# Convolution taps all on VectorE, the decay products a block pair later, and three steps of the mixers behind each gate chunk, in a hybrid decoder trunk

## The chip, the cores and the metric

The kernel runs on one core of a Trainium2 chip. The metric is device time in microseconds of one execution, and the median over several runs. Before the change three runs gave 1257.48, 1259.5 and 1262.86 us, a median of 1259.5 us.

A core has five engines that each work through their own list of instructions in order: TensorE (PE, whose weight loads the profile lists as PEld), VectorE (DVE), ScalarE (ACT), GpSimd (POOL) and SyncE (SP, which issues DMAs here). They wait for one another by semaphores.

## The reference

Two layers, 256 tokens, width 1024, all weights float32. Each layer is a half-step SwiGLU feed-forward, a mixing sub-layer with three branches, and a second feed-forward:

```python
for l in range(DEPTH):                                   # DEPTH = 2
    x = x + FFN_RESID * swiglu_ffn(rms_norm(x, ffn1_norm[l]), ffn1_w_in[l], ffn1_w_out[l])
    h = rms_norm(x, mix_norm[l])
    uv, c_q, c_kv, k_rope, z, xbc, dt_raw, gates = jnp.split(h @ w_in[l], IN_OFFSETS, axis=-1)
    y_a = gmlp_mixer(uv, ...)
    y_b = mla_mixer(c_q, c_kv, k_rope, cos, sin, ...)    # attention, 8 heads
    y_c = ssd_mixer(z, xbc, dt_raw, ...)                 # state-space scan
    g = jax.nn.sigmoid(gates).reshape(bsz, s, N_BRANCH, D_MODEL)
    merged = sum of g[:, :, i] * (y_i @ w_branch[l, i])
    x = x + merged @ w_out[l]
    x = x + FFN_RESID * swiglu_ffn(rms_norm(x, ffn2_norm[l]), ffn2_w_in[l], ffn2_w_out[l])
```

The state-space branch begins with a causal convolution over time with four taps, one filter for each of 1024 features, and a Silu. Its scan needs, for each of 8 heads and each of two chunks of 128 tokens, the decay matrix `exp(segsum(dt * a))`, a 128x128 triangle of exponentials of running sums:

```python
xbc = lax.conv_general_dilated(xbc, conv_w[:, None, :], (1,), [(SSD_CONV - 1, 0)], ...)   # SSD_CONV = 4
xbc = jax.nn.silu(xbc + conv_b)
dt = jax.nn.softplus(dt_raw + dt_bias)
lmat = jnp.exp(segsum(da))                               # da = dt * -exp(a_log)
```

## The kernel before, in words

**Products.** Every float32 weight chunk (128 partitions x up to 1024 columns, "sub") is loaded by SP into `raw` and split in two parts that TensorE takes at its fast rate: ACT casts the upper part (`whi`, L175) and DVE subtracts it to get the rest (`wlo`, L176). Four buffers hold each part, and the splits run three subs ahead of their use. A product is then three matmuls: L215 to L217 for feature-major results (128 features x 256 tokens), L221 to L223 for token-major ones (128 tokens x up to 512 columns). PE works in order, so a split that is late stops it.

**The mixing sub-layer**, function `mix`, has these stages on PE: eight 128-feature blocks of the convolution's input, in four pairs `i` (ps_in); two halves of the token-major v part (ps_v, 276 columns); seven steps `n` over pairs of middle blocks (`MID_PAIRS`; ps_in again: the latents of the attention for n < 3, then z and u); three and two sub-chunks for q and k/v; 24 chunks of the gates (ps_g); and the merge.

**The convolution.** DVE scales each pair of blocks into `xp` (L587, L589), ACT applies the last tap and the bias into `xbc`, and the other three taps are added in place. For the first block of each pair, `b == 0`, DVE does it with one instruction a tap (L596). For the second block POOL does it with two: a product into the tile `tap` (L599) and a sum (L600). ACT's Silu (L602) takes four blocks at a time. Behind it on ACT come the casts of later subs.

**The steps of the mixers.** All that is not a product with streamed weights is written as generators that yield, and `pump(n)` takes n steps of the first one in the list `work`. The state-space generator `ssd` has as its first step the softplus chain of small DVE instructions (L631 to L654), as its second the high and low parts of da (`dahi` L656, `dalo` L657), the products ps_s and ps_c (L667, L674), and then four steps that each make one decay product: `aseg` (L682, one half on DVE with `dahi`, one on POOL with `dalo`, three buffers), two matmuls into ps_sg (L687, L688) and ACT's exponential (L689). `pump(3)` stands behind each of the seven middle steps (L853), `pump(2 + n % 2)` behind each gate chunk `n` (L1037). By n = 2 the latents' squares are summed on POOL (L847) and turned over by the small product ps_css (L822). In the gate chunks the steps belong to the attention: POOL takes inverse roots for keys and queries (`rs_k`, `rs_q`, L301), multiplies the normed keys and queries (`qk`, L938 and L928), and PE transposes them (ps_t, L965).

**What sets the order.** The program states dependencies and buffers; a scheduler orders the instructions on each engine by its own estimate of time and by priority, where splits have high priority. So a step that is pumped elsewhere can also move instructions of other kinds. POOL issues its DMAs (the feed-forward's summed weights, L166, and accumulating ones, L169) in the same list as its arithmetic.

Of the kernel before, what the change touches and what calls it, by code (L numbers as in the profile page):

```python
# [10 lines left out]
F32 = mybir.dt.float32  # L11
# [4 lines left out]
ALU = mybir.AluOpType  # L16
# [3 lines left out]
P = 128  # L20
DEPTH = 2
SEQ = 256
# [86 lines left out]
def tile_trunk(ctx, tc, wst, xtok, xT, pos, pcol, prow, wsT, cst, out):  # L109
    nc = tc.nc  # L110
    act, dve, pool, pe = nc.scalar, nc.vector, nc.gpsimd, nc.tensor
# [4 lines left out]
    tp = ctx.enter_context(tc.tile_pool(name="tp", bufs=2))  # L116
# [5 lines left out]
    starts, o = [], 0  # L122
# [84 lines left out]
    def next_sub():  # L207
        i = st["use"]
        prefetch(AHEAD + 1)
        st["use"] += 1  # L210
        return splits.pop(i)

    def mm3(ps, whi, wlo, xhl, first, last):

        pe.matmul(ps, lhsT=whi, rhs=xhl[:, 0], start=first, stop=False)  # L215
        pe.matmul(ps, lhsT=whi, rhs=xhl[:, 1], start=False, stop=False)  # L216
        pe.matmul(ps, lhsT=wlo, rhs=xhl[:, 0], start=False, stop=last)  # L217

    def mm3x(ps, xhi, xlo, whi, wlo, first, last, again=False):

        pe.matmul(ps, lhsT=xhi, rhs=whi, start=first, stop=False, skip_group_check=again)  # L221
        pe.matmul(ps, lhsT=xhi, rhs=wlo, start=False, stop=False, skip_group_check=again)  # L222
        pe.matmul(ps, lhsT=xlo, rhs=whi, start=False, stop=last, skip_group_check=again)  # L223
# [89 lines left out]
    def halves(b):  # L313
        return slice(P * b, P * (b + 1))
# [231 lines left out]
    def mix(l, nrm, nxt, late, row, ws):  # L546
        col = pc[:, l]
        qn, kvn = col[:, 24:27], col[:, 27:29]
        cw = col[:, 29:61].rearrange("p (b i) -> p b i", i=4)
# [4 lines left out]
        def blocks(n=2):  # L554

            ps = acc.tile([P, 2, SEQ], F32, name="ps_in", tag="acc")
            for half in range(n):
                hi, lo = next_sub()
                for k in range(KD):
                    s = slice(P * k, P * (k + 1))  # L560
                    mm3(ps[:, half], hi[:, s], lo[:, s], nrm.hl[:, k], k == 0, k == KD - 1)
            return ps
# [3 lines left out]
        for i in range(4):  # L566
            if i == 0:

                pss = [acc.tile([P, SEQ], F32, name="ps_in", tag="acc") for _ in range(2)]
                subs = [next_sub() for _ in range(2)]  # L570
                for part in range(2):
                    for ps, (hi, lo) in zip(pss, subs):
                        for k in range(4 * part, 4 * part + 4):
                            s = slice(P * k, P * (k + 1))
                            mm3(ps, hi[:, s], lo[:, s], nrm.hl[:, k], k == 0, k == KD - 1)
                    if part == 0:
                        late()
                        nrm.finish(True)
                        R = nrm.R
                        R2 = R.unsqueeze(1).broadcast_to([P, 2, SEQ])  # L580
            else:
                ps = blocks()
            xp = tp.tile([P, 2, SEQ + 4], F32, name="xp", tag="xp")
            pool.memset(xp[:, :, 0:3], 0.0)
            if i == 0:
                for b in range(2):
                    dve.tensor_tensor(xp[:, b, 3 : SEQ + 3], pss[b], R, ALU.mult)  # L587
            else:
                dve.tensor_tensor(xp[:, :, 3 : SEQ + 3], ps, R2, ALU.mult)  # L589
            for b in range(2):  # L590
                f = 2 * i + b
                o = xbc[:, f]
                act.activation(o, xp[:, b, 3 : SEQ + 3], AF.Identity, scale=cw[:, f, 3:4], bias=cb_[:, f : f + 1])
                for w in range(3):
                    if b == 0:
                        dve.scalar_tensor_tensor(o, xp[:, b, w : w + SEQ], cw[:, f, w : w + 1], o, ALU.mult, ALU.add)  # L596
                    else:
                        c = tp.tile([P, SEQ], F32, name="tap", tag="sq")
                        pool.tensor_tensor(c, xp[:, b, w : w + SEQ], cw[:, f, w : w + 1].broadcast_to([P, SEQ]), ALU.mult)  # L599
                        pool.tensor_tensor(o, o, c, ALU.add)  # L600
        for i in range(2):
            act.activation(xbc[:, 4 * i : 4 * i + 4], xbc[:, 4 * i : 4 * i + 4], AF.Silu)  # L602
        xsT, bT, cT = xbc[:, 0:4], xbc[:, 4:6], xbc[:, 6:8]
# [4 lines left out]
        for half in range(2):  # L608
            pst = [acc.tile([P, VW], F32, name="ps_v", tag="acc") for _ in range(2)]
            k = 0  # L610
            for n in (3, 3, 2):
                hi, lo = next_sub()
                for i in range(n):
                    for b in range(2):
                        s, w = slice(P * b, P * (b + 1)), slice(VW * i, VW * (i + 1))
# [193 lines left out]
        def pump(n):  # L809
            while work and n > 0:  # L810
                try:
                    next(work[0])
                    n -= 1
                except StopIteration:
                    work.pop(0)

        def c_norm():
            ps = mxp.tile([P, 4], F32, name="ps_css", tag="mx")
            for i in range(2):
                for b in range(2):  # L820
                    c = 2 * i + b
                    pe.matmul(ps[:, c : c + 1], lhsT=css[:, i, P * b : P * (b + 1)], rhs=ones[:, 0:1], start=True, stop=True)  # L822
            m = tp.tile([P, 4], F32, name="ms_c", tag="ms4")
            dve.tensor_scalar(m[:, 0:2], ps[:, 0:2], 1.0 / 384, EPS, ALU.mult, ALU.add)
            dve.tensor_scalar(m[:, 2:4], ps[:, 2:4], 1.0 / 256, EPS, ALU.mult, ALU.add)
            r = tp.tile([P, 4], F32, name="rs_c", tag="rsc", bufs=1)
            pool.tensor_tensor(r, m, mhalf[:, :4], ALU.pow)
            return r

        for n, (a, b) in enumerate(MID_PAIRS):  # L830
            ps = blocks(b - a)[:, : b - a]
            Rn = R2[:, : b - a]
            if n < 3:
                cr = tp.tile([P, 2, SEQ], F32, name="craw", tag="t")
                dve.tensor_tensor(cr[:, : b - a], ps, Rn, ALU.mult)
                for k in range(a, b):
                    c = cr[:, k - a]
                    g = qn[:, k : k + 1] if k < 3 else kvn[:, k - 3 : k - 2]
                    act.activation(chi[:, k], c, AF.Copy, scale=g)
                    dve.scalar_tensor_tensor(clo[:, k], c, g, chi[:, k].bitcast(F32), ALU.mult, ALU.subtract)  # L840
                    to = css[:, 0 if k < 3 else 1]
                    if k in (0, 3):
                        act.activation(to, c, AF.Square)
                    else:
                        sq = tp.tile([P, SEQ], F32, name="csq", tag="sq")
                        act.activation(sq, c, AF.Square)
                        pool.tensor_tensor(to, to, sq, ALU.add)  # L847
            else:
                dve.tensor_tensor(zt[:, a - 5 : b - 5] if n < 5 else ut[:, a - 9 : b - 9], ps, Rn, ALU.mult)
            if n == 2:  # L850
                rc = c_norm()
            done["z"] = n >= 4
            pump(3)  # L853


        big = bp.tile([P, 2, 2, H, QK], F32, name="qk", tag="big12a")
# [5 lines left out]
        for k in range(3):  # L862
            hi, lo = next_sub()
            for b in range(2):
                s = slice(P * b, P * (b + 1))
                for i in range(2):
                    w = slice(384 * i, 384 * (i + 1))
                    mm3x(psq[b][i], chi[:, k, s], clo[:, k, s], hi[:, w], lo[:, w], k == 0, k == 2)
        for b in range(2):
            for i in range(2):  # L870
                o = q[:, b, 4 * i : 4 * i + 4].rearrange("p h d -> p (h d)")
# [6 lines left out]
        for k in range(2):  # L878
            hi, lo = next_sub()
            for b in range(2):  # L880
                s = slice(P * b, P * (b + 1))
                for i in range(2):
                    w = slice(512 * i, 512 * (i + 1))
# [142 lines left out]
        n = 0  # L1026
        for h in range(2):
            for i in range(3):
                ps = [acc.tile([P, HD], F32, name="ps_g", tag="acc") for _ in range(2)]
                for c in range(KD // 2):  # L1030
                    hi, lo = next_sub()
                    for kk_ in range(2):
                        k, w = 2 * c + kk_, slice(512 * kk_, 512 * (kk_ + 1))
                        for b in range(2):
                            s = halves(b)
                            mm3x(ps[b], nrm.hl[:, k, 0, s], nrm.hl[:, k, 1, s], hi[:, w], lo[:, w], k == 0, k == KD - 1)
                    pump(2 + n % 2)  # L1037
                    if n == 0:
                        work.insert(0, gmlp(ut))
                    n += 1  # L1040
                for b in range(2):
                    rcb = nrm.rc[:, b : b + 1]
                    if b == 0:
                        act.activation(sig[:, h, b, i], ps[b], AF.Copy, scale=rcb)
                    else:
                        dve.tensor_scalar(sig[:, h, b, i], ps[b], rcb, None, ALU.mult)
# [13 lines left out]
        for h in range(2):  # L1060
            hs = slice(HD * h, HD * (h + 1))
            for n, br in enumerate((0, 2, 1)):
                ps = [acc.tile([P, HD], F32, name="ps_br", tag="acc") for _ in range(2)]
                for c in range(2):
                    hi, lo = next_sub()
                    for i in range(2):
                        k, w = 2 * c + i, slice(512 * i, 512 * (i + 1))
# [15 lines left out]
        for h in range(2):  # L1083
            hs = slice(HD * h, HD * (h + 1))
            ps = [acc.tile([P, HD], F32, name="ps_out", tag="acc") for _ in range(2)]
            for c in range(KD // 2):
                hi, lo = next_sub()
                for i in range(2):
                    k, w = 2 * c + i, slice(512 * i, 512 * (i + 1))
# [20 lines left out]
    def late(first=nrm):  # L1110
        for j in range(KD):
            first.keep(j, x0[:, j])
        for h in range(2):
            first.squares(h)
# [135 lines left out]
```

## Time and profile before

| quantity | value |
|---|---|
| runs | 1257.48, 1259.5, 1262.86 us; median 1259.5 |
| profiled execution | 1265.08 us |
| its span, first to last instruction | 1263.4 us |
| granted TensorE clock, mean | 0.994 |
| PE busy | 1222.4 us, 97% of the span, 6236 matmuls |
| DVE busy | 905.8 us, 72%, 1223 instructions |
| ACT busy | 741.3 us, 59%, 1012 |
| POOL busy | 163.9 us, 13%, 176 |
| L599 and L600 on POOL, convolution of layer 0 | 11.6 + 12.3 us, 24 instructions |

A row of a view reads: line, engine, operation, output and inputs, tile sizes, number of instructions, then busy time in us, mean ns of one, and idle time ahead of it with what ended it. A row of the timeline has start, duration, engine, line; square brackets hold the idle time ahead and its releaser. A row of windows has a stretch of time, its length, the busy time of PE, PEld, DVE, ACT and POOL with the number of instructions, the granted clock, the DMA share and GB/s. In the convolution of layer 0 the stretch is 216 to 241.4 us, the decay products follow at 262 to 271, the attention's transposes at 334; layer 1 has the same at about 840, 880 and 952.

### The profile page before, as it was taken

How to read it: one execution, taken by the hardware profiler on the slowest of the kernel's cores; microseconds unless marked ns; L12 is line 12 of the kernel's file. 1: busy time of each engine (PE TensorE's matmuls, PEld its weight loads, DVE VectorE, ACT ScalarE, POOL GpSimd, SP SyncE). 2: the span in 40 equal slices, each digit the busy share in tenths (PEclk: the TensorE clock that was granted, in tenths of full speed). 3: DMA queues.
4: the chain of work that ended last, by engine and by line, in shares of the span. 5: the costliest groups of instructions: out<-in, count | busy, mean ns of one | idle time of the engine just before them, and what ended most of it. 6: DMA issues, size and time to landing. Idle time of an engine off the chain costs nothing.

```text
span 1263.4 us, 16844 instructions
## 1 busy us (share of the span) xinstructions
PE 1222.4 (97%) x6236; PEld 1025.8 (81%) x6236; DVE 905.8 (72%) x1223; ACT 741.3 (59%) x1012; POOL 163.9 (13%) x176
## 2 busy tenths in 40 slices
PE   6999999999999899999999999999999999999998
PEld 4788789989888678788888888898887877778886
DVE  5688755897856677876578885588886566878853
ACT  6567544656576476655566664457466654766642
POOL 2100001632400010000001000054242000100000
PEclk9999999999999999999999999999999999999999
DMA  9985664534744497886549655535375545885652
GB/s 330 311 260 184 209 193 146 185 129 164 258 168 165 140 282 224 259 268 211 183 167 321 223 186 202 185 125 197 108 220 182 162 161 182 271 243 192 216 188 80
DMA packets 71651, 255.17 MB, mean 202 GB/s; under 512 B 8080, under 2 KB 8208, under 8 KB 71440
## 3 DMA queue, kind: packets, MB, share of 16 engines
q1 hardware_dynamic: 61488, 219.40, 51.3%
q0 software_dynamic: 9216, 33.56, 10.8%
q10 hardware_dynamic: 864, 1.13, 0.3%
q8 instruction: 49, 0.80, 0.2%
q14 instruction: 34, 0.28, 0.1%
HBM read 253.01 MB, written 1.05 MB: 201 GB/s over the span
## 4 chain that ended last, share of the span: by engine, by line
PE 80%; DVE 7%; DMA 6%; ACT 2%; issue 2%; POOL 2%; SPq 0%; ACTq 0%; DVEq 0%
PE ps_out L223 7%; PE ps_out L221 7%; PE ps_out L222 7%; PE ps_in L222 6%; PE ps_in L223 6%; PE ps_in L221 6%; DMA raw<-in_w 4%; DVE wlo L176 3%; PE ps_g L223 3%; PE ps_g L222 3%; PE ps_g L221 3%; PE ps_in L217 2%; PE ps_in L215 2%; PE ps_in L216 2%; PE ps_wa L222 2%
## 5 line engine op out<-in xcount | busy, mean ns | idle before, releaser
L176 DVE TENSOR_TENSOR wlo<-raw,whi 128x1024 fp32r<-128x1024 f32 (+3 forms) x401 | 491.3, 1231 | 231.8 <-ACT whi L175 229.6
L175 ACT CAST whi<-raw 128x1024 fp32r<-128x1024 f32 (+3 forms) x401 | 414.3, 1038 | 316.3 <-PE ps_out L223 136.9
L222 PE MATMUL ps_in<-wlo,xg 128*128 128x512 f32 x448 | 177.5, 397 | 5.7 <-DVE wlo L176 5.7
L223 PE MATMUL ps_in<-whi,xg 128*128 128x512 f32 x448 | 175.5, 396 | 0.0
L221 PE MATMUL ps_in<-whi,xg 128*128 128x512 f32 x448 | 164.0, 399 | 9.1 <-ACT whi L175 8.0
L222 PEld LDWEIGHTS ps_in<-wlo,xg 128*128 128x128 f32 x448 | 84.8, 189 | 27.6 <-DVE wlo L176 9.8
L221 PEld LDWEIGHTS ps_in<-whi,xg 128*128 128x128 f32 x448 | 82.9, 189 | 27.9 <-ACT whi L175 10.5
L223 PEld LDWEIGHTS ps_in<-whi,xg 128*128 128x128 f32 x448 | 84.6, 190 | 17.1
L217 PE MATMUL ps_in<-xg,wlo 128*128 128x256 f32 x336 | 96.5, 289 | 1.5 <-DVE wlo L176 1.5
L216 PE MATMUL ps_in<-xg,whi 128*128 128x256 f32 x336 | 96.2, 288 | 0.0
L215 PE MATMUL ps_in<-xg,whi 128*128 128x256 f32 x336 | 95.1, 289 | 0.3 <-ACT whi L175 0.2
L222 PE MATMUL ps_g<-wlo,xg 128*128 128x512 f32 x192 | 75.9, 395 | 0.0
L222 PE MATMUL ps_out<-wlo,aa 128*128 128x512 f32 x192 | 75.7, 394 | 0.0
L223 PE MATMUL ps_out<-whi,aa 128*128 128x512 f32 x192 | 75.4, 393 | 0.0
L221 PE MATMUL ps_out<-whi,aa 128*128 128x512 f32 x192 | 75.2, 392 | 0.0
L223 PE MATMUL ps_g<-whi,xg 128*128 128x512 f32 x192 | 75.1, 391 | 0.0
L221 PE MATMUL ps_g<-whi,xg 128*128 128x512 f32 x192 | 72.8, 394 | 0.0
L217 PEld LDWEIGHTS ps_in<-xg,wlo 128*128 128x128 f32 x336 | 65.4, 195 | 1.9 <-DVE wlo L176 1.9
L216 PEld LDWEIGHTS ps_in<-xg,whi 128*128 128x128 f32 x336 | 65.4, 195 | 0.7 <-issue 0.3
L215 PEld LDWEIGHTS ps_in<-xg,whi 128*128 128x128 f32 x336 | 64.5, 195 | 1.2 <-ACT whi L175 1.1
L221 PE MATMUL ps_out<-whi,ab 128*128 128x512 f32 x160 | 62.2, 389 | 0.0
L222 PE MATMUL ps_out<-wlo,ab 128*128 128x512 f32 x160 | 62.2, 389 | 0.0
(324 smaller groups left out, 2416.9 us busy)
## 6 DMA issues: line engine op xcount, KB each, us to landing
raw<-in_w SPq DMA_DIRECT2D x397, 512.0 KB, 4.2
xsum<-in_w POOLq DMA_DIRECT2D x32, 512.0 KB, 6.9
ysum<-in_w POOLq DMA_DIRECT2D x32, 512.0 KB, 8.1
raw<-in_w SPq DMA_DIRECT2D x8, 414.0 KB, 3.2
raw<-in_w SPq DMA_DIRECT2D x6, 384.0 KB, 3.0
raw<-in_w SPq DMA_DIRECT2D x4, 276.0 KB, 2.9
x<-in_xT SPq DMA_DIRECT2D x4, 256.0 KB, 7.8
x<-in_x SPq DMA_DIRECT2D x1, 1024.0 KB, 16.8
```

The costliest lines, as they stand in the source:

```text
L175: act.copy(hi[:, a:b], r[:, a:b])
L176: dve.tensor_tensor(lo[:, a:b], r[:, a:b], hi[:, a:b].bitcast(F32), ALU.subtract)
L215: pe.matmul(ps, lhsT=whi, rhs=xhl[:, 0], start=first, stop=False)
L216: pe.matmul(ps, lhsT=whi, rhs=xhl[:, 1], start=False, stop=False)
L217: pe.matmul(ps, lhsT=wlo, rhs=xhl[:, 0], start=False, stop=last)
L221: pe.matmul(ps, lhsT=xhi, rhs=whi, start=first, stop=False, skip_group_check=again)
L222: pe.matmul(ps, lhsT=xhi, rhs=wlo, start=False, stop=False, skip_group_check=again)
L223: pe.matmul(ps, lhsT=xlo, rhs=whi, start=False, stop=last, skip_group_check=again)
```

## The change

1. All three taps of both blocks are DVE's; the tile `tap` and POOL's two instructions a tap are gone. That is 24 more DVE instructions and 48 fewer on POOL in the two layers.
2. The seven middle steps pump 2, 3, 3, 3, 3, 4, 3 steps instead of 3 each: 21 in both cases, but the 3rd, 6th, 9th, 12th and 15th step now come behind the next pair of blocks. The 3rd is the first decay product, the 6th the fourth.
3. Each gate chunk pumps three steps instead of two and three by turns.

```diff
                 for w in range(3):
-                    if b == 0:
-                        dve.scalar_tensor_tensor(o, xp[:, b, w : w + SEQ], cw[:, f, w : w + 1], o, ALU.mult, ALU.add)
-                    else:
-                        c = tp.tile([P, SEQ], F32, name="tap", tag="sq")
-                        pool.tensor_tensor(c, xp[:, b, w : w + SEQ], cw[:, f, w : w + 1].broadcast_to([P, SEQ]), ALU.mult)
-                        pool.tensor_tensor(o, o, c, ALU.add)
+                    dve.scalar_tensor_tensor(o, xp[:, b, w : w + SEQ], cw[:, f, w : w + 1], o, ALU.mult, ALU.add)
...
             done["z"] = n >= 4
-            pump(3)
+            pump((2, 3, 3, 3, 3, 4, 3)[n])
...
-                    pump(2 + n % 2)
+                    pump(3)
```

Below the first edit the lines of the changed kernel are five lower: L682 becomes L677, L687 and L688 become L682 and L683, L928 becomes L923; the tap L596 becomes L595. The order in the feed-forward stages is the same in both kernels.

On DVE, from the second xp of layer 0's convolution, before:

```order
L589 TENSOR_TENSOR xp<-ps_in,R 128x2x256
L596 SCALAR_TENSOR_TENSOR xbc<-xp,pc,xbc 128x256
L176 TENSOR_TENSOR wlo<-raw,whi 128x1024
L596 SCALAR_TENSOR_TENSOR xbc<-xp,pc,xbc 128x256 x2
L176 TENSOR_TENSOR wlo<-raw,whi 128x828
L596 SCALAR_TENSOR_TENSOR xbc<-xp,pc,xbc 128x256 x2
L589 TENSOR_TENSOR xp<-ps_in,R 128x2x256
L176 TENSOR_TENSOR wlo<-raw,whi 128x828
```

and in the changed kernel, from its last xp to the split of 828 columns for the second half of ps_v (ahead of it stand two xp of one block, two more xp, twelve taps, and splits of 1024 four times, 828 twice, 552 once):

```order
L589 TENSOR_TENSOR xp<-ps_in,R 128x2x256
L595 SCALAR_TENSOR_TENSOR xbc<-xp,pc,xbc 128x256 x2
L176 TENSOR_TENSOR wlo<-raw,whi 128x828
L595 SCALAR_TENSOR_TENSOR xbc<-xp,pc,xbc 128x256 x7
L176 TENSOR_TENSOR wlo<-raw,whi 128x828
```

The splits keep their places among the blocks, with up to seven taps between two of them where there were at most three.

On DVE at the decay products of layer 0 (aseg: one half of a decay product; craw, yhl: the latents), before:

```order
L682 TENSOR_TENSOR aseg<-cs,dahi 128x512 x3
L176 TENSOR_TENSOR wlo<-raw,whi 128x1024
L840 SCALAR_TENSOR_TENSOR yhl<-craw,pc,yhl 128x256 x2
L835 TENSOR_TENSOR craw<-ps_in,R 128x256
L682 TENSOR_TENSOR aseg<-cs,dahi 128x512
```

and in the changed kernel:

```order
L677 TENSOR_TENSOR aseg<-cs,dahi 128x512 x3
L176 TENSOR_TENSOR wlo<-raw,whi 128x1024
L835 SCALAR_TENSOR_TENSOR yhl<-craw,pc,yhl 128x256 x2
L176 TENSOR_TENSOR wlo<-raw,whi 128x1024
L830 TENSOR_TENSOR craw<-ps_in,R 128x256
L677 TENSOR_TENSOR aseg<-cs,dahi 128x512
```

One more split stands ahead of the fourth product. On PE the first step product ps_s now has 142 ps_in matmuls of the middle blocks ahead of it instead of 125, and from ps_c to the fourth decay product there are 21 instead of 26, so that the fourth has 12 more ahead of it in all; the ps_css products, which stood behind it, are now ahead of it.

On POOL in layer 1, from the sums' DMAs to the attention's products, before:

```order
L166 DMA xsum<-in_w 128x1024 x2
L169 DMA xsum<-in_w 128x1024
L938 TENSOR_TENSOR qk<-qk,gg 128x8x64
L169 DMA xsum<-in_w 128x1024
L301 TENSOR_TENSOR rs_k<-ms_k,mhalf 128x16
L301 TENSOR_TENSOR rs_q<-ms_q,mhalf 128x16
L928 TENSOR_TENSOR qk<-qk,rs_k 128x8x64 x2
```

and in the changed kernel:

```order
L166 DMA xsum<-in_w 128x1024 x2
L169 DMA xsum<-in_w 128x1024 x2
L933 TENSOR_TENSOR qk<-qk,gg 128x8x64
L301 TENSOR_TENSOR rs_k<-ms_k,mhalf 128x16
L923 TENSOR_TENSOR qk<-qk,rs_k 128x8x64 x2
L301 TENSOR_TENSOR rs_q<-ms_q,mhalf 128x16
```

The second accumulating DMA has moved ahead of the first qk product, and rs_q behind the two others. In layer 0 rs_k and rs_q keep their places ahead of them; there the first accumulating DMA, which stood ahead of the mask of the gMLP's weights (L290), now stands between the mask and the first qk product.

## The prediction

> **What bounds the kernel now.** I read the page first: which engine fills the span, and which engines stand on the chain of work that ended last.
>
> ```profile
> PE 1222.4 (97%) x6236; PEld 1025.8 (81%) x6236; DVE 905.8 (72%) x1223; ACT 741.3 (59%) x1012; POOL 163.9 (13%) x176
> PE 80%; DVE 7%; DMA 6%; ACT 2%; issue 2%; POOL 2%; SPq 0%; ACTq 0%; DVEq 0%
> ```
>
> TensorE (PE) is at work for 97% of the span, and the change neither adds nor removes a matmul. So it can act only through the few moments in which PE waits, and through PE's clock. The second view is PE's waits, with two rows of its weight loads (PEld): total us, times, longest.
>
> ```profile
> PE ps_in L221 <- ACT whi L175: 8.0, 6, 2.9
> PE ps_in L222 <- DVE wlo L176: 5.7, 7, 1.5
> PE ps_sg L687 <- DVE aseg L682: 4.5, 2, 2.2
> PE ps_v L222 <- DVE wlo L176: 2.6, 2, 1.3
> PE ps_t L965 <- POOL qk L928: 1.8, 1, 1.8
> PE ps_in L217 <- DVE wlo L176: 1.5, 2, 0.8
> ...
> PEld ps_v L222 <- DVE wlo L176: 3.4, 4, 1.5
> PEld ps_in L217 <- DVE wlo L176: 1.9, 2, 1.0
> ```
>
> The first two rows belong to the feed-forward stages, whose order is the same in both kernels; I leave them as they are. What the change can touch are the other four: the splits behind the convolution (ps_v, ps_in L217; 2.6 + 1.5 = 4.1 us over both layers), the decay product (4.5 us), and the keys of the second layer's attention (1.8 us).
>
> The third view is stretches of layer 0 and one of layer 1. After each window's length come PE, PEld, DVE, ACT and POOL busy, then PE's granted clock.
>
> ```profile
> 216.00:241.40 25.40, 24.10 (x195) 23.68 (x194) 24.97 (x26) 12.92 (x19) 23.11 (x26) 1.00 0.46 137
> 268.00:271.40 3.40, 1.15 (x9) 0.90 (x7) 3.40 (x5) 1.60 (x5) 1.52 (x3) 1.00 0.35 116
> 271.50:274.90 3.40, 3.40 (x16) 3.40 (x17) 3.17 (x7) 2.73 (x6) 1.57 (x2) 0.50 0.43 116
> 889.30:892.70 3.40, 3.40 (x16) 3.40 (x17) 3.17 (x7) 2.74 (x6) 1.57 (x2) 0.50 0.33 116
> ```
>
> In the convolution DVE is busy 24.97 of 25.40 us and POOL 23.11: both are full, and PE waits for DVE behind it. The stretch with the decay stall is followed, in both layers, by 3.4 us at half clock. At half rate these cost half their length, 1.7 us each.
>
> **Taps on DVE.** 24 pairs on POOL (three taps for one block of each of the four pairs, both layers) go, 24 DVE taps come: 12 more in this window. The question is the duration of a tap.
>
> ```profile
> L596 DVE SCALAR_TENSOR_TENSOR xbc<-xp,pc,xbc 128x256 f32<-128x256 f32 x12 | 10.1, 862 | 0.1
> L176 DVE TENSOR_TENSOR wlo<-raw,whi 128x1024 fp32r<-128x1024 f32 x4 | 6.5, 1651 | 0.3 <-ACT whi L175 0.3
> L176 DVE TENSOR_TENSOR wlo<-raw,whi 128x828 fp32r<-128x828 f32 x4 | 5.0, 1242 | 0.0
> L589 DVE TENSOR_TENSOR xp<-ps_in,R 128x512 f32<-128x512 f32 x3 | 2.0, 677 | 0.0
> ...
> L760 DVE SCALAR_TENSOR_TENSOR zt<-zt,pc,spr_y x8: 471/474/476, 305.5 to 924.4; 128x256 f32<-128x256 f32 x8
> ...
> 270.56 1.21 DVE L176 TENSOR_TENSOR wlo<-raw,whi 128x1024 fp32r<-128x1024 f32 x1
> ```
>
> L760 is the same operation on the same tile size, and POOL does nothing beside it: 0.474 us, always. Beside a busy POOL a tap takes 0.862, and a split 1.651 where it takes 1.21 elsewhere. So the two engines hold each other up, and taking POOL away pays for the taps: 24 × 0.474 = 11.4 us where 12 × 0.862 = 10.3 stood. [...]
>
> Now the walk to the split that PE waited for:
>
> ```profile
> 229.90 0.28 PE L216 MATMUL ps_in<-xg,whi 128*128 128x256 f32 x1
> 230.02 0.28 PE L217 MATMUL ps_in<-xg,wlo 128*128 128x256 f32 x1
> 240.32 0.39 PE L222 MATMUL ps_v<-wlo,xg 128*128 128x276 f32 x1 [1.30 <-DVE wlo L176]
> ...
> 215.46 0.76 DVE L587 TENSOR_TENSOR xp<-ps_in,R 128x256 f32<-128x256 f32 x2 [1.82 <-PE ps_in L217]
> ...
> 269.96 0.68 DVE L682 TENSOR_TENSOR aseg<-cs,dahi 128x512 fp32r<-128x512 f32 x1
> ```
>
> PE ends its last convolution block at 230.3 and wants the split at 240.32 − 1.30 = 239.02. In the new order DVE has, from 215.46 to its last xp, 0.76, two wider xp (2 × 0.68), twelve taps and seven splits (four of 1024, two of 828, one of 552; 1.21 scaled by columns gives 0.98 and 0.65): 0.76 + 1.36 + 5.69 + 4.84 + 1.96 + 0.65 = 15.3 us. Each instruction starts about 0.08 before its predecessor's row ends (269.96 + 0.68 against the 270.56 above), so 23 × 0.08 = 1.8 comes off: 229.0. So the last xp waits some 1.3 for PE and starts at 230.3. Then come xp, two taps, a split of 828, seven taps, and the split of 828 in question: 0.68 + 9 × 0.474 + 2 × 0.98 = 6.9, less 0.9. It lands at 236.3, 2.7 us early. Both stalls of the convolution vanish. The PE rows say 4.1 us, the weight-load rows 3.4 + 1.9 = 5.3; I take the middle, **4.7**.
>
> The second Silu (L602) now waits for DVE's last tap instead of POOL's; it is not on PE's path here.
>
> **The decay products.** The tuple gives two steps instead of three behind the first block pair. In the order, PE has 12 more ps_in matmuls and the four ps_css products ahead of the fourth decay product, and DVE one more split.
>
> ```profile
> 265.59 2.06 DVE L176 TENSOR_TENSOR wlo<-raw,whi 128x1024 fp32r<-128x1024 f32 x1
> ...
> 270.78 0.47 PE L687 MATMUL ps_sg<-aseg,upr 128*128 128x512 f32 x1 [2.25 <-DVE aseg L682]
> ...
> 271.32 0.70 PE L822 MATMUL ps_css<-cs,css 128*128 128x1 f32 x4
> 271.88 0.56 PE L217 MATMUL ps_in<-xg,wlo 128*128 128x256 f32 x1
> ```
>
> A ps_in matmul takes 0.12 us (230.02 − 229.90 above, where PE is not waiting), ps_css 0.56 (271.88 − 271.32). PE asks 12 × 0.12 + 0.56 = 2.0 later; DVE delivers 1.21 − 0.08 = 1.13 later. The stall of 2.25 becomes 2.25 − 2.0 + 1.13 = 1.4, a gain of 0.85 per layer, **1.7** in both. Bounds: if the added split takes 2.06, as the one beside POOL at 265.59, the stall is 2.3 and the gain −0.1; if the stall vanishes, 4.5.
>
> **The half clock.** Two rows say how long a stall may be:
>
> ```profile
> 954.28 0.64 PE L965 MATMUL ps_t<-cs,qk 128*96 128x128 f32 x4 [1.75 <-POOL qk L928]
> 955.40:958.80 3.40, 3.40 (x16) 2.81 (x16) 2.01 (x3) 2.30 (x3) 0.00 (x0) 1.00 0.42 160
> ```
>
> Behind a stall of 1.75 the clock stayed at 1.00; behind the two of 2.25 it fell. At 1.4 it should stay, worth 2 × 1.7 = 3.4 at most, 0 at least. I take half, **1.7**: only the profiled run shows these windows, its 1265.08 us are 5.6 above the median of the timed runs (1259.5), and I can't tell whether those carry them.
>
> **Three steps behind each gate chunk.** In layer 1 POOL's order becomes rs_k, the two qk products, rs_q; in layer 0 one accumulating DMA now stands behind the mask L290 and ahead of L938.
>
> ```profile
> 940.05 5.59 POOL L301 TENSOR_TENSOR rs_k<-ms_k,mhalf 128x16 f32<-128x16 f32 x1 [3.37 <-DVE ms_k L299]
> 945.62 2.90 POOL L301 TENSOR_TENSOR rs_q<-ms_q,mhalf 128x16 f32<-128x16 f32 x1
> 948.49 5.73 POOL L928 TENSOR_TENSOR qk<-qk,rs_k 128x512 f32<-128x512 f32 x2
> ...
> 320.01 0.88 POOL L169 DMA_DIRECT2D xsum<-in_w  x1
> 320.79 3.83 POOL L301 TENSOR_TENSOR rs_k<-ms_k,mhalf 128x16 f32<-128x16 f32 x1
> 324.60 4.71 POOL L301 TENSOR_TENSOR rs_q<-ms_q,mhalf 128x16 f32<-128x16 f32 x1
> 329.28 2.48 POOL L928 TENSOR_TENSOR qk<-qk,rs_k 128x512 f32<-128x512 f32 x2
> ...
> 334.19 0.82 PE L965 MATMUL ps_t<-cs,qk 128*96 128x128 f32 x6
> ```
>
> Layer 1: L928 ends 2.90 earlier than 954.22, and the stall of 1.75 goes: **1.75** (0 at least, if the long rows only trade places). Layer 0: the DMA's 0.9 falls on the chain, L928 ends about 332.7, PE asks at 334.19, so the remaining 1.5 us cover it. Queued behind L928 there are only the sums' DMAs for the next feed-forward.
>
> **The sum.** 4.7 + 1.7 + 1.7 + 1.75 = 9.85, against the profiled 1265.08: 1255.2, and taken off the median of the runs, 1249.6. With the lower ends 4.1 − 0.1 + 0 + 0 = 4.0 (1255.5); with the upper 5.3 + 4.5 + 3.4 + 1.75 = 14.95 (1244.5).
>
> **Rivals.** *B: the decay stall keeps its size and its half clock.* DVE's splits around it are as slow as 2.06 us, since POOL's own decay products still run beside them. Then 4.7 + 1.75 = 6.45: 1253. For it: the bound above. Against it: only one of the splits in that stretch takes 2.06, the next 1.21.
>
> *C: DVE becomes the bound.* If the tap takes 0.862 and the split 1.651 for a reason of their own (chained updates of one tile, not POOL), then the 21 taps ahead of the split cost 21 × 0.388 = 8.1 more, the eight wide splits 4 × 0.44 + 4 × 0.26 = 2.8 more, less the 1.3 that DVE would wait at the last xp and the 2.7 in hand. A stall of 6.9 instead of 2.35 per layer: 9.1 us in both, 3.4 for two new half-clock windows, less 1.75: 1259.5 + 10.8 = 1270. It decides once the lateness passes 4.0 + 2.35 us, a tap of about 0.474 + 6.35 / 21 = 0.78. For it:
>
> ```profile
> L596 DVE SCALAR_TENSOR_TENSOR xbc<-xp,pc,xbc x24: 715/838/958, 221.8 to 855.8; 128x256 f32<-128x256 f32 x24
> ```
>
> no tap has been seen under 0.715. Against it: POOL was busy 23.11 of the 25.40 us around them, and L760's 0.474.
>
> *D: the attention's POOL chain is late.* If layer 0's chain takes layer 1's durations (5.59 + 2.90 + 5.73 = 14.2 against 11.0), 3.2 + 0.9 less the margin 2.4 gives a new stall of 1.7, and if layer 1 keeps its own, the gain is 8.1 − 1.7 = 6.4: 1253.
>
> *E: the half clock does not come from the stalls.* The windows stay; 9.85 − 1.7 = 8.15: 1251. [...]
>
> **Chances.** Forecast 50%, B 20%, C 10%, D 10%, E 10%. The range that holds 8 of 10 reaches from the upper sum, 1244, over B and D with the spread of a few runs to 1257. What can be told from no change is about 0.5%, 6.3 us: faster means under 1253.2. The forecast's own range, 1245 to 1255, puts 46 of its 50 there; B and D lie on the bound, and give half, 15 of 30; E 8 of 10. Faster 0.69. Slower over 0.5% comes from C alone, 0.08. Same 0.23.
>
> **What would show it.** In the changed trace: taps of about 0.47 us and no PE wait for wlo at ps_v (right) or taps over 0.7 (C); a wait at the fourth ps_sg of 1.0 to 1.8 (right), 2.2 or more with 0.50 behind it (B); no wait at ps_t in either layer (right), one in layer 0 (D); clock 1.00 throughout the middle blocks (right), 0.50 without a stall ahead (E). I would be wrong altogether if a new wait stood first on PE, as for the second Silu or for the last exp, that the old order did not have.

## The result, and the profile after

| | before | after |
|---|---|---|
| median of 6 runs each | 1260.28 us | 1250.54 us |
| lowest and highest | 1257.48, 1265.32 | 1248.88, 1253.42 |
| profiled execution | 1265.08 us | 1250.70 us |
| its span | 1263.4 us | 1248.7 us |

The ratio is 0.9926, 95% interval 0.9908 to 0.9943: 9.7 us faster, where 9.85 were forecast. The sum came out; its terms did not. The kernel after, first its busy times and then four rows of PE's waits (total us, times, longest; the first two rows belong to the feed-forward stages):

```profile
PE 1217.8 (98%) x6236; PEld 1024.6 (82%) x6236; DVE 899.7 (72%) x1247; ACT 741.5 (59%) x1012; POOL 113.1 (9%) x128
...
PE ps_in L221 <- ACT whi L175: 6.7, 4, 2.3
PE ps_in L222 <- DVE wlo L176: 4.1, 5, 1.5
PE ps_t L960 <- POOL qk L923: 2.9, 2, 2.2
PE ps_sg L682 <- DVE aseg L677: 1.0, 2, 0.5
```

The two rows of the convolution (ps_v, ps_in L217) are gone. The decay product's wait went from 4.5 to 1.0 us. The attention's (ps_t) grew from 1.8 to 2.9 us, and both waits in it are now in layer 0. DVE has 24 instructions more and is busy 6 us less. The groups of DVE in layer 0's convolution, and all the taps of the program:

```profile
L595 DVE SCALAR_TENSOR_TENSOR xbc<-xp,pc,xbc 128x256 f32<-128x256 f32 x24 | 10.3, 476 | 0.0
L176 DVE TENSOR_TENSOR wlo<-raw,whi 128x1024 fp32r<-128x1024 f32 x6 | 7.2, 1221 | 0.6 <-ACT whi L175 0.6
...
L595 DVE SCALAR_TENSOR_TENSOR xbc<-xp,pc,xbc x48: 470/475/480, 219.3 to 850.4; 128x256 f32<-128x256 f32 x48
```

A tap takes 0.475 us in all 48 cases, where 0.862 was the mean before, and 24 taps take 10.3 us of DVE where 12 took 10.1. A split of 1024 columns fell from 1.651 to 1.221.

The timeline of the kernel after shows the fourth decay product on DVE and PE, and what is new, the keys' products on POOL in layer 0 and PE's waits for them:

```profile
265.37 0.67 DVE L677 TENSOR_TENSOR aseg<-cs,dahi 128x512 fp32r<-128x512 f32 x1
266.19 0.47 PE L682 MATMUL ps_sg<-aseg,upr 128*128 128x512 f32 x1 [0.49 <-DVE aseg L677]
...
320.09 8.81 POOL L301 TENSOR_TENSOR rs_q<-ms_q,mhalf 128x16 f32<-128x16 f32 x1 [0.45 <-DVE ms_q L299]
328.87 2.06 POOL L923 TENSOR_TENSOR qk<-qk,rs_k 128x512 f32<-128x512 f32 x2
...
329.96 0.31 PE L960 MATMUL ps_t<-cs,qk 128*96 128x128 f32 x1 [2.17 <-POOL qk L923]
330.99 0.64 PE L960 MATMUL ps_t<-cs,qk 128*96 128x128 f32 x4 [0.71 <-POOL qk L923]
```

rs_q, a tile of 128x16, holds POOL for 8.81 us, and the keys' products stand behind it. The next view is windows of the kernel after; the granted clock stands behind the five engines' busy times:

```profile
262.29:265.70 3.41, 3.41 (x27) 3.12 (x26) 3.41 (x5) 1.63 (x6) 1.41 (x2) 1.00 0.36 115
265.70:269.11 3.41, 2.92 (x22) 2.81 (x22) 2.81 (x7) 3.41 (x7) 1.58 (x2) 1.00 0.42 120
328.48:331.89 3.41, 1.21 (x7) 0.98 (x8) 2.95 (x4) 0.55 (x2) 2.45 (x3) 1.00 0.00 0
331.89:335.30 3.41, 3.41 (x9) 2.65 (x9) 3.41 (x5) 1.56 (x3) 0.00 (x0) 0.50 0.65 183
```

The clock stays at 1.00 around the decay product, and falls to 0.50 behind the new wait in the attention.

### The profile page after: what moved, and what is told of

Its sections match the earlier page's. It is cut to its first block, busy times and chain, and to the rows that moved or that the text cites. A ratio compares the mean times of both kernels' runs of the same rounds, so it can differ in the third digit from the quotient of the medians.

```text
span 1248.7 us, 16800 instructions
## 1 busy us (share of the span) xinstructions
PE 1217.8 (98%) x6236; PEld 1024.6 (82%) x6236; DVE 899.7 (72%) x1247; ACT 741.5 (59%) x1012; POOL 113.1 (9%) x128
## 3 DMA queue, kind: packets, MB, share of 16 engines
q10 hardware_dynamic: 864, 1.13, 0.3%
HBM read 253.01 MB, written 1.05 MB: 203 GB/s over the span
## 4 chain that ended last, share of the span: by engine, by line
PE 68%; DVE 3%; DMA 1%; ACT 1%; issue 1%; POOL 0%; ACTq 0%; DVEq 0%
PE ps_out L223 6%; PE ps_out L221 6%; PE ps_out L222 6%; PE ps_in L222 6%; PE ps_in L223 6%; PE ps_in L221 6%; PE ps_g L222 3%; PE ps_g L223 3%; PE ps_g L221 3%; PE ps_wa L222 2%; PE ps_wa L223 2%; PE ps_wa L221 2%; PE ps_in L215 2%; PE ps_in L216 2%; PE ps_br L221 2%; PE ps_in L217 2%
## 5 line engine op out<-in xcount | busy, mean ns | idle before, releaser
L176 DVE TENSOR_TENSOR wlo<-raw,whi 128x1024 fp32r<-128x1024 f32 (+3 forms) x401 | 483.4, 1210 | 231.9 <-ACT whi L175 229.4
L222 PE MATMUL ps_in<-wlo,xg 128*128 128x512 f32 x448 | 178.0, 398 | 4.3 <-DVE wlo L176 4.1
L222 PEld LDWEIGHTS ps_in<-wlo,xg 128*128 128x128 f32 x448 | 85.2, 190 | 26.0 <-DVE wlo L176 8.2
L217 PE MATMUL ps_in<-xg,wlo 128*128 128x256 f32 x336 | 94.5, 283 | 0.0
L222 PE MATMUL ps_g<-wlo,xg 128*128 128x512 f32 x192 | 76.4, 398 | 0.0
L222 PE MATMUL ps_out<-wlo,aa 128*128 128x512 f32 x192 | 75.7, 394 | 0.0
L217 PEld LDWEIGHTS ps_in<-xg,wlo 128*128 128x128 f32 x336 | 64.0, 191 | 0.3
L216 PEld LDWEIGHTS ps_in<-xg,whi 128*128 128x128 f32 x336 | 64.0, 191 | 0.1
L215 PEld LDWEIGHTS ps_in<-xg,whi 128*128 128x128 f32 x336 | 63.1, 191 | 1.0 <-issue 0.7
L223 PE MATMUL ps_out<-whi,ab 128*128 128x512 f32 x160 | 62.3, 389 | 0.0
L221 PE MATMUL ps_out<-whi,ab 128*128 128x512 f32 x160 | 62.3, 389 | 0.0
```

Of the source, the lines that this page charges most:

```text
L176: dve.tensor_tensor(lo[:, a:b], r[:, a:b], hi[:, a:b].bitcast(F32), ALU.subtract)
```

## The experiments

### The three edits one by one

The orders of instructions had more to say than the prediction took from them. With the first edit alone, ACT, POOL and SP have the order of the whole change row for row, and DVE has it but for a few rows late in the scan; on PE ps_s already has 142 ps_in ahead of it, and POOL in layer 1 already has rs_q behind the keys' products. With the third edit alone, the order on all five engines is that of the kernel before. So the three were run apart.

First edit alone, against the kernel after:

```diff
-            pump((2, 3, 3, 3, 3, 4, 3)[n])
+            pump(3)
...
-                    pump(3)
+                    pump(2 + n % 2)
```

> Only the first edit: all taps on DVE, the middle steps and the gate chunks pumped as before. The order of this kernel is that of the whole change on DVE, ACT, SP and POOL around the decay products and the attention; on PE the fourth decay product has four ps_in matmuls more and the ps_css products (0.56 us) less ahead of it. Theory 1 (the taps move everything): no wait behind the convolution, taps of 0.47 us, a wait at the fourth ps_sg of about 0.6 us instead of 2.25 with the clock at 1.00 behind it, no wait at ps_t in layer 1, the new wait of some 2.9 us at ps_t in layer 0: about 1250.5 us, ratio 0.9925. Rival (the prediction's accounting, in which the tuple brings the decay's and the clock's part): 4.7 us for the convolution and 1.75 for the attention at most, 1253 to 1256, ratio 0.995 to 0.997.

Measured: 1249.84 us, ratio 0.9921 (0.9906 to 0.9935). Two rows of PE's waits:

```profile
PE ps_t L960 <- POOL qk L923: 2.1, 2, 1.4
PE ps_sg L682 <- DVE aseg L677: 0.9, 2, 0.5
```

There is no row for the convolution, and both waits at ps_t are in layer 0. The taps alone bring the whole gain; the prediction's accounting, which gives parts of it to the other two edits, falls.

Second edit alone, against the kernel before:

```diff
             done["z"] = n >= 4
-            pump(3)
+            pump((2, 3, 3, 3, 3, 4, 3)[n])
```

> Only the second edit: the middle steps pumped 2, 3, 3, 3, 3, 4, 3, taps as before. On DVE the order at the decay products is that of before; on PE the fourth has two ps_in less and the four ps_css products ahead of it. Theory 1: the waits behind the convolution stay (4.1 us), the wait at the fourth ps_sg becomes 2.25 + 0.24 - 0.56 = 1.9 us, the half clock may stay or go, and the wait at ps_t in layer 1 goes, since POOL's order there is that of the change: 1256 to 1260 us, ratio 0.997 to 1.0. Rival (the prediction's accounting): decay 1.7 and clock 1.7 to 3.4, 1255 or less.

Measured: 1260.43 us, ratio 1.0007 (0.9995 to 1.0019). PE's waits:

```profile
PE ps_v L222 <- DVE wlo L176: 2.6, 2, 1.3
PE ps_sg L687 <- DVE aseg L682: 2.4, 2, 1.2
PE ps_t L965 <- POOL qk L928: 2.0, 2, 1.3
PE ps_css L822 <- POOL css L847: 1.2, 2, 0.6
```

The decay wait fell from 4.5 to 2.4 (1.2 per layer, where 1.9 was expected), and 1.2 of it came back at ps_css, which now stands ahead and waits for POOL. The wait at ps_t left layer 1 (1.75) and came up in layer 0 (1.3 + 0.7). What the tuple gives it takes elsewhere: no gain.

Third edit alone, against the kernel before:

```diff
-                    pump(2 + n % 2)
+                    pump(3)
```

> Only the third edit: three steps of the mixers behind each gate chunk, all else as before. The order of its instructions is the same as that of before on all five engines, so this is a kernel that can't differ but by the spread of the runs. Theory 1 (the third edit does nothing): the waits of before, 1259 to 1261.5 us, ratio 0.9985 to 1.0015. Rival (the prediction, which gave this edit the wait at ps_t in layer 1): 1.75 us less, ratio 0.9986 at most.

Measured: 1260.34 us, ratio 0.9999 (0.9984 to 1.0014). PE's waits are those of before:

```profile
PE ps_sg L687 <- DVE aseg L682: 4.5, 2, 2.2
PE ps_v L222 <- DVE wlo L176: 2.6, 2, 1.3
PE ps_t L965 <- POOL qk L928: 1.7, 1, 1.7
```

The edit moves no instruction and no time. It also shows how far two kernels of one and the same order agree: to 0.15%.

### POOL kept busy beside the taps

The whole change, with as much work for POOL as before, a product and a sum for each tap of the second blocks, into a tile that nothing reads:

```diff
                     dve.scalar_tensor_tensor(o, xp[:, b, w : w + SEQ], cw[:, f, w : w + 1], o, ALU.mult, ALU.add)
+                    if b == 1:
+                        c = tp.tile([P, SEQ], F32, name="tap", tag="sq")
+                        pool.tensor_tensor(c, xp[:, b, w : w + SEQ], cw[:, f, w : w + 1].broadcast_to([P, SEQ]), ALU.mult)
+                        pool.tensor_tensor(c, c, xp[:, b, w : w + SEQ], ALU.add)
```

> The whole change, and POOL still does a product and a sum per tap of each second block, into a tile that nothing reads: the order on DVE is unchanged. Theory 1 (POOL and DVE hold each other up on operations with two inputs from SBUF): DVE's taps take 0.8 us or more, its splits of 1024 columns in the convolution 1.6, PE waits 5 to 7 us per layer behind the convolution, and the kernel is slower than the one before: 1262 to 1272 us, ratio 1.002 to 1.01. Rival (a tap takes 0.47 whoever works beside it, and 0.86 was a matter of the old order): taps of 0.47, 1250.5 us, ratio 0.9925.

On PE, DVE, ACT and SP the order came out as that of the whole change, row for row.

Measured: 1265.17 us, ratio 1.0033 (1.0014 to 1.0051), 14.6 us more than the whole change. DVE's groups in layer 0's convolution, all its taps, and PE's wait:

```profile
L595 DVE SCALAR_TENSOR_TENSOR xbc<-xp,pc,xbc 128x256 f32<-128x256 f32 x22 | 15.1, 736 | 0.0
L176 DVE TENSOR_TENSOR wlo<-raw,whi 128x1024 fp32r<-128x1024 f32 x4 | 6.4, 1650 | 0.3 <-ACT whi L175 0.3
...
L595 DVE SCALAR_TENSOR_TENSOR xbc<-xp,pc,xbc x48: 469/826/961, 219.0 to 863.6; 128x256 f32<-128x256 f32 x48
...
PE ps_v L222 <- DVE wlo L176: 10.7, 4, 4.1
```

With the same order on DVE, the median tap goes from 0.475 to 0.826 and the split from 1.221 to 1.650. So it is POOL's work beside them that makes them long, and not the chained updates of one tile that rival C assumed. The cost of C does come with it: 5.3 us of waits per layer (C had 6.9), and a kernel slower than the one before. DVE's xp, which reads ps_in, takes no longer for it: 0.676 us for a pair of blocks (L589) here, 0.685 in the whole change.

### Only the last block's taps moved

The kernel before, with three of POOL's twelve taps per layer moved to DVE:

```diff
-                    if b == 0:
+                    if b == 0 or i == 3:
```

> The kernel before, with one block in eight moved: only the last block's three taps go from POOL to DVE. The order on PE and POOL is else that of before, at the decay products and in the attention too; on DVE one tap more stands ahead of the split that PE waited for, two behind it. So POOL and DVE still slow each other down, but POOL's last sum comes some 6 us earlier. Theory S (the decay products were late because ACT's second Silu waited 4.0 us for POOL's last sum and held up the casts behind it): ACT's wait there falls under 1 us, the fourth decay product's wait from 2.25 to at most 1.0 us with no half clock behind it, the wait at ps_in L217 (0.75) goes, the wait at ps_v grows from 1.3 to about 2.2; 1253 to 1257 us, ratio 0.995 to 0.998. Rival (the decay products gain by the new order, or by DVE free of POOL in the whole convolution): the wait at ps_sg stays 2.0 or more; 1259 to 1262 us, ratio 0.999 to 1.001.

Measured: 1253.58 us, ratio 0.995 (0.9932 to 0.9968). By the medians that is 7.4 us of the 9.7, by a quarter of the moved taps; by the ratios it is 6.3 (4.0 to 8.6) of 9.3. On PE, ACT and SP the order is that of the kernel before, row for row. ACT's second Silu in the kernel before and in this one, then of this one PE's decay wait, its fourth decay product, and the window of the ps_v stage:

```profile
241.96 1.06 ACT L602 ACTIVATE xbc<-xbc 128x1024 f32<-128x1024 f32 x1 [4.01 <-POOL xbc L600]
...
237.39 1.06 ACT L602 ACTIVATE xbc<-xbc 128x1024 f32<-128x1024 f32 x1 [1.88 <-DVE xbc L596]
...
PE ps_sg L687 <- DVE aseg L682: 4.5, 2, 2.3
...
265.38 0.68 DVE L682 TENSOR_TENSOR aseg<-cs,dahi 128x512 fp32r<-128x512 f32 x1
266.20 0.76 PE L687 MATMUL ps_sg<-aseg,upr 128*128 128x512 f32 x1 [2.25 <-DVE aseg L682]
...
227.72:240.33 12.61, 12.61 (x99) 12.23 (x98) 10.72 (x17) 8.36 (x14) 5.18 (x7) 1.00 0.55 182
```

Theory S falls: ACT waits 2.1 us less, and the decay product is as late as ever, 2.25 us. PE and DVE move together as long as the order is that of before. The rival is right on that, and wrong on the time, since both waits of the convolution vanished, the one at ps_v too, which I expected to grow. With POOL done earlier, the last taps and splits run alone: the shortest tap is 0.468. The ps_v stage takes 12.61 us, where it took 14.25 before and takes 12.14 with the whole change. So it is POOL's last 6 us that cost this stage most.

### rs_q behind the keys' products

The whole change, with one buffer for the tiles rs_k and rs_q, so that rs_q has to wait until rs_k is read. PE's order is that of the whole change; on POOL in layer 0, rs_q stands behind the keys' products.

```diff
-        r = tp.tile([P, n], F32, name=f"rs_{name}", tag=f"rs{n}")
+        r = tp.tile([P, n], F32, name=f"rs_{name}", tag=f"rs{n}", bufs=1 if n == 16 else None)
```

> The whole change, and one buffer instead of two for the inverse roots rs_k and rs_q, so that rs_q (8.8 us on POOL in layer 0) stands behind the products of the keys in layer 0 too; PE's order is unchanged. Theory 1: the wait of 2.2 + 0.7 us at ps_t in layer 0 goes, and with it the 3.4 us at half clock behind it (1.7): about 4.6 us less than the whole change, 1246 us, ratio 0.989. Rival: POOL is slowed there whatever it does, the products of the keys take the time that rs_q took, and the wait stays over 1.5 us: 1249 to 1251.

Measured: 1247.46 us, ratio 0.9894 (0.9878 to 0.9911), 3.1 us less than the whole change's median. PE has no wait at ps_t any more. POOL in layer 0:

```profile
314.82 3.23 POOL L301 TENSOR_TENSOR rs_k<-ms_k,mhalf 128x16 f32<-128x16 f32 x1
318.12 2.18 POOL L923 TENSOR_TENSOR qk<-qk,rs_k 128x512 f32<-128x512 f32 x2
323.75 4.61 POOL L301 TENSOR_TENSOR rs_q<-ms_q,mhalf 128x16 f32<-128x16 f32 x1 [3.45 <-DVE qk L926]
```

The keys' products end 5.5 us after rs_k starts; in the kernel after, rs_q stands between and it is 14.5 us (316.42 to 330.93). The 4.6 us expected were 2.9 of waits and 1.7 of half clock. The waits of 2.9 are gone, but PE now waits 0.5 for a split in the same stretch (ps_g L222). The granted clock, 0.9945 in the mean of the whole change's runs, is 0.99525 here, which is worth 0.9 us of some 1250: 2.4 + 0.9 = 3.3, against 3.1 measured.

The same edit on the kernel with the taps alone:

```diff
-            pump((2, 3, 3, 3, 3, 4, 3)[n])
+            pump(3)
...
-        r = tp.tile([P, n], F32, name=f"rs_{name}", tag=f"rs{n}")
+        r = tp.tile([P, n], F32, name=f"rs_{name}", tag=f"rs{n}", bufs=1 if n == 16 else None)
...
-                    pump(3)
+                    pump(2 + n % 2)
```

> The first edit alone, with one buffer for rs_k and rs_q, so that rs_q stands behind the products of the keys in layer 0: the second and third edit left out of the fastest kernel so far. Theory 1 (they bring nothing): the waits and the time of the kernel with all three edits and one buffer, 1246 to 1248.5 us, ratio 0.989 to 0.991. Rival (the tuple helps once the taps are on DVE, as it takes 0.2 to 0.5 us off the waits at the decay products): 1248.5 us or more.

Measured: 1247.27 us, ratio 0.9894 (0.9867 to 0.9922), the same. The taps and the one buffer are all that is needed; the other two edits can be left out. These two kernels are the fastest here.

## Why the prediction was right, and where it was not

**The sum** of 9.85 us against 9.7 came out by luck in part: the terms for the convolution and the decay products were too small, and a wait in the attention that was put at nothing came.

**The tap and the convolution** held. A tap of 0.474 was forecast, 0.475 came; the last xp waits 0.79 for PE (1.3 forecast); both waits vanished. The sentence that the second Silu "is not on PE's path here" holds for the changed kernel. What the walk left out is the second of the two waits (ps_in L217): it said that both vanish, and followed only the first. In the kernel before, that wait hangs on POOL through ACT: the Silu waits 4.01 us for POOL's last sum (241.96, above), the copy of a ps_v result and a cast stand behind it on ACT, and DVE's splits wait for that cast:

```profile
244.37 3.68 DVE L176 TENSOR_TENSOR wlo<-raw,whi 128x1024 fp32r<-128x1024 f32 x3 [3.04 <-ACT whi L175]
```

The size was taken from rows of waits only, 4.1 to 5.3 us, and that is too small, as the lengths of the stages below show.

**The decay products** were mis-sized and put down to the wrong edit. The step was "PE asks 2.0 later, DVE delivers 1.13 later": a wait of 1.4. It came to 0.49, a gain of 3.5 us in both layers, not 1.7; rival B, in which it keeps its size, is out. DVE's part held: from the end of the third product to the end of the fourth it takes 6.1 us after (259.94 to 266.04), 5.0 before. The step assumed that DVE's softplus chain moves with PE. It moved ahead of PE. The windows from the end of the convolution on PE to the exponential in that chain, for the kernel before, the one with the last block moved, and the kernel after:

```profile
230.30:252.90 22.60, 20.39 (x158) 19.54 (x158) 18.29 (x29) 16.15 (x22) 11.23 (x13) 1.00 0.63 202
...
227.88:248.30 20.42, 20.07 (x158) 19.48 (x158) 17.39 (x32) 16.12 (x21) 5.02 (x7) 1.00 0.65 214
...
229.20:247.40 18.20, 18.20 (x149) 18.20 (x148) 15.31 (x32) 15.46 (x19) 0.00 (x0) 1.00 0.70 229
```

PE has done 158 matmuls by then with the order of before, whether ACT waits long or not, and 149 with the order of the change: nine matmuls of 0.12, about 1.1 us. On ACT the second Silu stands two casts and two copies of ps_v results later in the changed order. With this the step comes to 2.25 − 2.0 + 1.13 − 1.1 = 0.3, an estimate, against 0.49. That the order decides is shown by two runs: with POOL kept busy and the order of the change, the convolution waits 5.3 us per layer and the decay product 0.5; with the last block moved and the order of before, the convolution does not wait and the decay product waits 2.25. Which row of the order does it, ACT's place for the Silu or another, was not run apart and stays open. And this order came with the taps, by the scheduler, not with the tuple.

**The half clock** was priced at 1.7, half of what could be gained, because the forecast could not tell. In the profiled runs both windows behind the decay product went, worth 3.4 us, and one came behind the attention's new wait, 1.7, which was not forecast; so this figure, too, was hit by luck. Over 33 runs of the kernel before the granted clock is 0.9930 in the mean, over 6 of the changed one 0.9945: 0.0015 of some 1260 us, 1.9 us. Rival E falls for these windows, since they went and came with the waits. But the reading that a stall of 1.75 is short enough and one of 2.25 too long does not hold as it stands; the last section has what the traces show instead.

**The attention** is the miss of kind. The wait in layer 1 went (1.75) as forecast, but by the order that the first or the second edit brings, and not by the third, which does nothing: the rival that the change doesn't do what it says, for one edit in three, was not on the list. In layer 0 a new wait came, as rival D had it, though not by layer 1's durations. The step that failed is "the remaining 1.5 us cover it": it took rs_q at the 4.71 of its row before, and it took 8.81. The wait of 2.9 us and 1.7 of half clock are more than the 1.75 gained in layer 1.

**The account.** The rows of waits give 4.1 for the convolution, 3.5 for the decay product and −1.1 for the attention, and the clock 1.9: 8.4 of the 9.7 us. The lengths of the stages on PE give more. The ps_v stage and the middle steps up to q, in layer 0, of the kernel before (layer 1 has the same within 0.01 us):

```profile
230.14:244.39 14.25, 12.79 (x99) 12.15 (x97) 11.10 (x14) 7.86 (x13) 11.39 (x13) 1.00 0.53 167
244.39:296.60 52.21, 49.21 (x394) 47.40 (x395) 45.63 (x85) 30.53 (x47) 13.69 (x11) 0.97 0.45 150
```

and of the kernel after:

```profile
229.00:241.14 12.14, 12.14 (x98) 12.14 (x97) 10.49 (x19) 9.32 (x13) 0.00 (x0) 1.00 0.62 208
241.14:288.60 47.46, 46.97 (x397) 45.74 (x396) 42.40 (x83) 28.22 (x44) 12.23 (x11) 1.00 0.48 152
```

The ps_v stage is 2.1 us shorter per layer, where its row of waits has 1.3; the other 0.8 lies between matmuls, where the view lists no wait. The middle steps are 4.75 shorter, of which 1.7 is half clock in the profiled run. Without it they give 6.1 in both layers: 3.5 of the decay product, 1.5 of the wait at ps_in L217, and 1.1 more. So the convolution was worth at least 4.2 + 1.5 = 5.7 us, not 4.7. With the clock and the attention the sum is 4.2 + 6.1 + 1.9 − 1.1 = 11.1. The measured 9.7 has an interval from 7.2 to 11.6, and two profiled executions of one order, that of the kernel before and of the third edit alone, are 3.4 us apart (1263.4 and 1260.0); the terms are not known better than that. Too little by 2.8 for the convolution and the decay products and too much by 2.9 for the attention: that is what cancelled. DVE did not become the bound (C), because no POOL work was left beside its taps.

## What to carry to other kernels

Where two engines slow each other, price a moved operation by a row where the other engine is idle (a tap took 0.826 us beside POOL's work and 0.475 without it), and look for the wait of a third engine on the tail of the removed queue: a quarter of the moved taps gave more than half of the gain. Where a scheduler sets the order, look at the order that each edit gives alone before crediting a term to it; here one edit of three made the whole difference and one moved nothing. A tiny operation in an in-order queue ahead of work that PE waits for is to be priced by its worst row (8.81 us for rs_q, a tile of 128x16), not by its size.

## What the runs showed of the hardware

**The half-clock windows lie on one grid.** In the kernel before, half clock sets in at 29.12, 59.84, 271.47, 889.28 and 1261.33 us: 9, 62, 181 and 109 times 3.413 apart. In the kernel after it sets in at 14.45, 28.11, 58.83, 331.89 and 1246.66 us: 4, 9, 80 and 268 times. In both traces each of these windows lasts 3.413 us, but for the last, which the program's end cuts off. What goes with a fall is how long PE works within the grid's window ahead. In these two traces the seven windows at full clock in which PE worked for 0.37 to 1.21 us were all followed by half clock; of the seven with 1.78 to 1.92 us three were; of those with more, none. Windows of the grid, each with the one behind it, of the kernel before:

```profile
950.72:954.13 3.41, 1.81 (x11) 1.26 (x9) 2.61 (x3) 0.69 (x1) 3.41 (x2) 1.00 0.79 232
954.13:957.54 3.41, 3.26 (x17) 2.78 (x18) 1.61 (x2) 2.09 (x4) 0.10 (x1) 1.00 0.75 268
```

of the run with the tuple alone:

```profile
266.06:269.47 3.41, 1.83 (x11) 1.59 (x12) 3.41 (x5) 1.51 (x5) 1.53 (x3) 1.00 0.45 115
269.48:272.89 3.41, 3.41 (x17) 3.32 (x16) 3.18 (x7) 2.90 (x6) 1.75 (x2) 0.50 0.35 115
429.90:433.31 3.41, 1.61 (x7) 1.08 (x8) 3.41 (x6) 1.00 (x3) 0.00 (x0) 1.00 0.43 154
433.32:436.73 3.41, 3.41 (x9) 2.64 (x9) 0.94 (x2) 0.00 (x0) 0.00 (x0) 0.50 0.46 154
```

and of the run with the taps alone:

```profile
423.12:426.53 3.41, 1.83 (x8) 1.30 (x9) 3.41 (x5) 0.83 (x2) 0.00 (x0) 1.00 0.45 157
426.54:429.95 3.41, 3.41 (x17) 2.81 (x16) 1.32 (x3) 1.05 (x1) 0.00 (x0) 1.00 0.41 150
```

Behind 1.21 (the attention's new wait) and 1.61 us of work the clock fell; behind 1.81 and 1.83 it stayed in two cases and fell in one. The length of a wait does not tell either: behind the 1.75 us in the attention of layer 1 of the kernel before the clock stayed at 1.00, and with the tuple alone it fell to 0.50 behind the decay product of layer 0, where the wait is 1.2 us. Whether the place of a wait on the grid decides was not tried apart. The clock also goes with the scatter between runs of one kernel: of the 14 runs of the kernel before that stand beside the first four experiments, the fastest (1256.59) has a granted clock of 0.997 and the slowest (1265.13) one of 0.989, and a line through all gives 1.05 us for each 0.001 of clock and takes up 85% of the variance. Through the 19 runs beside the last three experiments it is 0.80 us and 38%.

**One small operation on POOL takes 2.9 to 8.8 us.** rs_q, the same 128x16 tile and instruction, took 4.71 and 2.90 us in the two layers before, 8.81 and 2.94 after, 8.22 and 2.94 with the taps alone, the tuple alone and POOL kept busy, and 4.61 and 6.83 with one buffer. In the traces of the kernel before and after, DVE was at work for all of it, but for the 8.81, where it was for 6.04; whether it is DVE that holds it up, and with which operation, was not tried.
